# A hybrid decoder step on one core: attention heads taken in another order of steps, and one page more scored among the last pairs

## The chip, the cores and the metric

The kernel runs on one core of one Trainium2 chip. The metric is the device time of one execution in microseconds (us). TensorE (PE in the rows, its weight loads PEld) multiplies matrices into PSUM; VectorE (DVE), ScalarE (ACT) and GpSimd (POOL) work on tiles; SyncE (SP) and POOL issue most of the DMAs.

## The reference

One layer of a decoder for 512 prompt rows and 8 sample rows, model width 2048. Cut to what the change touches:

```python
q, k, v, lf                      # 8 heads of 128, 512 rows; q and k after an RMS norm, lf a log forget value
F = cumsum(lf)
s = q @ k.T * 128 ** -0.5 + F[:, None] - F[None, :]      # in blocks of 128 queries, causal
y = softmax(s) @ v
# for each of the 8 sample rows: the same over 2 pages of 128 cached keys and itself
s_sample = sum(q_row * cache_k[page_table[b]], -1) * scale + forget terms
```

Ahead of this stand the projections of the normalised input (`w_in`), behind it `w_proj_b`, `w_out` and a gated feed-forward part. Every product is made in three parts of reduced precision: weights and data are split into a high and a low tile (`wh`, `wl`, and so on), ACT casting the high one, DVE subtracting for the low one.

## The kernel before

**Order of the work.** Most products are "pairs": two weight chunks make seven products of 8 x 3 matmuls (about 2.9 us of TensorE each). `run_pairs` (L326) runs over steps `t`, seven to a unit; at each step it issues the small work that is due (`take`, `ahead`, and what the dictionary `late` has for `t`), then the product. A weight part is split two products ahead of its use. The units of the first mixer's late part are 23: step 161 is where they end, and `t0` is step 147. Engines T, V and S are wrapped by `Ordered` (L53; its line is L60, which is why most rows say L60): they keep the program's order. In the next stage G and Y (POOL and SP) keep it too.

**The stage around the change** (from L1618) is a loop over 16 half chunks of eight remaining gate columns, `for n, (j, e) in enumerate(halves)` (L1898), with 8 steps `k` in each: 128 steps of six matmuls. After the six matmuls of step `8 n + k` it runs what the dictionary `plan` holds for that step, in the order in which `put` (L1817) was called: first the heads in their order, then the sample rows' work. At k = 2 ACT casts the weights of the half after next, at k = 4 DVE makes their low part, at k = 3 SP loads those of four halves on.

**A head** has 13 steps (`HP`, L1832) and starts at step b = 1 + 13 hh. Its work: `f_load` and `f_roots` (SP: q, k and their two rows of roots, and v), `f_norm` (DVE), `f_forget` (a matmul, then ACT), `f_split` (ACT) and `f_split_low` (DVE) for q and k, `f_values` (4 transposes, then ACT) and `f_values_low` (DVE), `f_scores` for the four blocks (`fS`), `f_max` (DVE, then ACT's exponential), `f_scale` (DVE: reciprocal and multiply), three `f_turn` (transposes into `fPT`, then ACT's cast `fph`), three `f_turn_low` (DVE: `fpl`), four `f_attend` (`fy`), `f_result` (ACT). Block 3 is the longest and the last; every `f_turn` reads a part of it. The tail of a head lies beside the start of the next one.

**Buffers.** All these PSUM results, and those of the sample rows, share four one-bank buffers (`pm`, L75, `mm_ps`). `st` tiles are 33, `pt` tiles 9, weight tiles `raw` 7, `wh` and `wl` 3 each.

**Pages.** The sample rows' scores are 16 pages' worth of work. `s_load` (L1437) fetches a broadcast query row `qb` (SP) and two key tiles by indirect DMA (POOL); `s_scores` (L1457) has two parts. A page with i < `PT` (L1447) lies in three `pt` tiles, and each part is a multiply and a reduction over 512 columns. A later page lies in one `raw` tile: part 0 is a multiply, part 1 a reduction over 1024 columns. Pages 0 to 3 are scored among the last pairs (`pages`, L1574), the other twelve in the stage, 11 steps to two pages, from step 8 to step 70.

**Later**, at L2210, the pairs of `w_out` have at step 9 (second unit, its third product) `log_exp` (L108), which has ACT load the table with the logarithm and the exponential.

Of the kernel before, what the change touches and what calls it, by code (L numbers as in the profile page):

```python
# [18 lines left out]
P = 128  # L19
# [4 lines left out]
N = SEQ + NS  # L24
# [39 lines left out]
def tile_hybrid_step(ctx: ExitStack, tc: tile.TileContext, I, O):  # L64
    nc = tc.nc
    S, V, G, T, Y = nc.scalar, nc.vector, nc.gpsimd, nc.tensor, nc.sync
# [13 lines left out]
    def nm(s):  # L80
        uid[0] += 1
        return f"{s}{uid[0]}"
# [4 lines left out]
    def mconst(shape, name, dt=F32, tag=None):  # L87
        return cm.tile(shape, dt, tag=tag or name, name=name)

    def st(name, dt=F32):  # L90
        return sp.tile([P, 528], dt, tag="s", name=nm(name))

    def pt(name, dt=F32):
        return sp.tile([P, 528], dt, tag="p", name=nm(name), bufs=9)

    def tiny(name):
        return tp.tile([P, 32], F32, tag="tiny", name=nm(name), bufs=12)
# [7 lines left out]
    def dram(shape, name):  # L105
        return dp.tile(shape, F32, tag=nm(name), name=nm(name))
# [48 lines left out]
    def raw_tile():  # L155
        return wp.tile([P, 1024], F32, tag="raw", name=nm("raw"), bufs=7)

    def wraw(src):
        raw = raw_tile()
        with tc.high_priority():  # L160
            nc.sync.dma_start(raw[:, :src.shape[1]], src)
        return raw
# [12 lines left out]
    def on(f, *a):  # L175
        return lambda: f(*a)
# [51 lines left out]
    def parts_of(t):  # L228

        return t[:, :HN], t[:, HN:2 * HN]  # L230
# [496 lines left out]
    for i, (c0, n) in enumerate(phases):  # L727
        todo = {j: [] for j in range(NPRE)}

        def put(j, f, *a):  # L730
            todo[j].append(on(f, *a))
# [13 lines left out]
        if i + 1 < len(phases):  # L745
            a, b = range(c0 + n, c0 + 2 * n)
# [113 lines left out]
    for e in range(2):  # L860
        t = mconst([P, NS * NPG], f"idxf{e}")
# [5 lines left out]
    def gather(dst, src, idx):  # L867
        return G.indirect_dma_start(dst, None, src, bass.IndirectOffsetOnAxis(ap=idx, axis=0))
# [348 lines left out]
    H = mheads = follows = None  # L1217
# [95 lines left out]
    dv = dram([FH, P, N], "dv")  # L1313
# [123 lines left out]
    def s_load(i):  # L1437
# [3 lines left out]
        Y.dma_start(qb[:, :512], dqf[e, b].partition_broadcast(P))  # L1441
        kps = [pt("kp")[:, :512] for _ in range(NPG)] if i < PT else raw_tile().rearrange("p (g n) -> p g n", g=NPG)
        W.k[i] = qb, kps
        for g in range(NPG):
            gather(kps[g] if i < PT else kps[:, g], I["cache_k"], idx_h[e][:, b * NPG + g:b * NPG + g + 1])

    PT = 5  # L1447

    class Pages:
        pass  # L1450
# [6 lines left out]
    def s_scores(i, part):  # L1457
        e, b = divmod(i, NS)
        qb, kps = W.k[i]
        if i < PT:  # L1460
            V.tensor_tensor(kps[part], kps[part], qb[:, :512], op=ALU.mult)
# [15 lines left out]
    dss, drr = dram([2, FH, N], "dss"), dram([2, FH, N], "drr")  # L1477
# [4 lines left out]
            Y.dma_start(t[:, :N], src)  # L1482

    def f_roots(H):
        H.rq, H.rk, H.v = st("fi"), st("fi"), st("fi")
        for t, src in ((H.rq, drr[0, H.i].partition_broadcast(P)), (H.rk, drr[1, H.i].partition_broadcast(P)),
                       (H.v, dv[H.i])):
            Y.dma_start(t[:, :N], src)

    def f_norm(H):  # L1490
        for t, w, r in ((H.q, qwc, H.rq), (H.k, nkw, H.rk)):
            V.scalar_tensor_tensor(t[:, :N], t[:, :N], w, r[:, :N], op0=ALU.mult, op1=ALU.mult)
        H.rq = H.rk = None
# [5 lines left out]
    for hh in range(FH):  # L1499
        H = Head()  # L1500
        H.i, H.p, H.pt, H.fs, H.sm, H.tp = hh, [], {}, {}, {}, {}
        heads.append(H)
    H = None
# [27 lines left out]
    t0, tq = 7 * (len(units) - 2), 7 * (2 * FH)  # L1531
# [3 lines left out]
    def gate_load(n):  # L1535
        if n < len(halves):
            j, e = halves[n]
            gw[n] = raw_tile()
            Y.dma_start(gw[n], I["w_in"][1 + 24 + 24 + KC + j][:, e * 1024:(e + 1) * 1024])
# [13 lines left out]
    def gate_split(n):  # L1553
        gate_cast(n)
        gate_low(n)
# [3 lines left out]
    def upper():  # L1559
# [8 lines left out]
    late_steps = {7 * (KC + 2): late_turn, tq + 2: root_load, tq + 5: root_make, tq + 8: rows_load, tq + 11: rows_make,  # L1568
                  tq + 15: lambda: (s_rows(0), s_rows(1)), t0 + 9: lambda: (hX.pop(5), f_load(heads[0]), f_roots(heads[0]), upper()),
                  t0 + 8: lambda: (gate_load(0), gate_load(1)),  # L1570
                  t0 + 10: lambda: (gate_load(2), gate_load(3)), t0 + 12: on(s_load, 4),
                  t0 + 11: on(gate_split, 0), t0 + 13: lambda: (gate_split(1), f_norm(heads[0]))}
    late_steps = {t: [f] for t, f in late_steps.items()}
    pages = ((133, 143), (140, 150), (147, 157), (152, 162))  # L1574
    for i, (a, b) in enumerate(pages):
        for t, f in ((a, on(s_load, i)), (b, on(s_scores, i, 0)), (b + 2, on(s_scores, i, 1))):
            late_steps.setdefault(t, []).append(f)
# [6 lines left out]
    for j in range(KC):  # L1584
# [11 lines left out]
        if j < NG:  # L1596
            t = sgs[j]
            V.tensor_tensor(z2(t), acc, z2(t), op=ALU.mult)
        else:
            t = pt("pao")  # L1600
# [11 lines left out]
    for n in (7, 4):  # L1612
        for i in range(8):
            t = st("hf", F32R)
# [4 lines left out]
    G, Y = (Ordered(tc, e) for e in (G, Y))  # L1619
# [70 lines left out]
    def f_max(H, i):  # L1690
        n = (i + 1) * P
        ps = H.fs.pop(i)
        s = st("fs")
        sm = tiny("sm")
        V.tensor_tensor_reduce(s[:, :n], ps[:, :n], H.nf[:, :n], -1.0, 3e38, ALU.add, ALU.min, sm[:, 0:1])
        S.activation(s[:, :n], s[:, :n], AF.Exp, bias=sm[:, 0:1], scale=-1.0, accum_out=sm[:, 1:2])
        H.p.append(s)
        H.sm[i] = sm
        if i == NB - 1:
            H.q = H.k = H.v = H.qr = H.kr = H.nf = None  # L1700

    def f_scale(H, i):
        n = (i + 1) * P
# [129 lines left out]
    for hh, H in enumerate(heads):  # L1833
        b = 1 + hh * HP
        if hh:
            put(max(1, b - 11), f_load, H)
            put(max(2, b - 8), f_roots, H)
            put(b, f_norm, H)
        put(b + 1, f_forget, H)
        put(b + 2, f_split, H)  # L1840
        put(b + 3, f_values, H)
        put(b + 4, f_split_low, H)
        put(b + 4, f_keys_out, H)
        put(b + 5, f_values_low, H)
        for s, i in ((8, 0), (9, 1), (11, 2), (12, 3)):
            put(b + s, f_scores, H, i)
            put(b + s + 1, f_max, H, i)
            put(b + s + 3, f_scale, H, i)
        for j in range(3):
            put(b + 17 + j, f_turn, H, j)  # L1850
            put(b + 18 + j, f_turn_low, H, j)
        for j in range(NB):
            put(b + min(21 + j, 23), f_attend, H, j)
        put(b + 24, f_result, H)
        put(max(100 + 3 * hh // 1, b + 25), y_split, hh)
        put(max(100 + 3 * hh // 1, b + 25) + 1, y_low, hh)
    put(3, s_offsets)
    put(5, s_keep)
    for i in range(4, 16):
        b = 8 + 11 * (i - 4) // 2  # L1860
        if i > 4:
            put(max(1, b - 11), s_load, i)
        put(b, s_scores, i, 0)
        put(b + 2, s_scores, i, 1)
# [8 lines left out]
    for n in range(8):  # L1873
        t = 83 + 5 * n
# [10 lines left out]
    H = None  # L1885
    mg = [None] * KC
# [37 lines left out]
    T, V, S, G, Y = nc.tensor, nc.vector, nc.scalar, nc.gpsimd, nc.sync  # L1924
# [6 lines left out]
    def hl_parts(pool, tag, src, n=N):  # L1931
        hi, lo = (pool.tile([P, 528], F32R, tag=tag, name=nm("mf")) for _ in range(2))
        S.copy(hi[:, :n], src[:, :n])
        V.tensor_tensor(lo[:, :n], src[:, :n], hi[:, :n].bitcast(F32), op=ALU.subtract)
        return [(hi[:, o:o + HN], lo[:, o:o + HN]) for o in (0, HN)]
# [10 lines left out]
    def quarters(i):  # L1946
        return [t[:, o:o + HN] for t in (mg[i], mg[8 + i]) for o in (0, HN)]

    def m_sums(i, part):
        b11, b12, b21, b22 = quarters(i)  # L1950
        if part == 0:
            V.tensor_tensor(b11, b11, b12, op=ALU.subtract)
            V.tensor_tensor(b12, b22, b12, op=ALU.subtract)
        if part == 1:
            V.scalar_tensor_tensor(b22, b22, -1.0, b11, op0=ALU.mult, op1=ALU.subtract)
        if part == 2:
            V.scalar_tensor_tensor(b21, b22, -1.0, b21, op0=ALU.mult, op1=ALU.subtract)

    def m_parts(i, n):
        if n == 5:  # L1960
            mX[5][i], mX[7][i] = hl_parts(hp, "hl", mg[i])
            return
        f = quarters(i)[3 if n == 6 else 2]
        t = (st if i == 7 else pt)("mf", F32R)
        hi, lo = mX[n][i] = parts_of(t)
        S.copy(hi, f)
        V.tensor_tensor(lo, f, hi.bitcast(F32), op=ALU.subtract)
        if i < 7:
            G.dma_start(dxf[i + 8 * (n == 4)][:, :N], t[:, :N])
# [182 lines left out]
    def load2(u, o, e):  # L2152
        raws[u, o, e] = wraw(I["w_fi"][u + o * KF][:, e * 1024:(e + 1) * 1024])
# [21 lines left out]
    for n in (6, 4):  # L2175
        for i in range(7):
            t = st("mf", F32R)
# [3 lines left out]
    def fetch_xa(cs):  # L2181
        for c in cs:
            xa[c] = st("xa")
            nc.sync.dma_start(xa[c][:, :N], dxa[c])
# [18 lines left out]
    def first_weights(o):  # L2203
        ws.append(parts2(0, o, 0))
        load2(1, o, 0)
# [1 line left out]
    r2 = st("rr")  # L2207
    run_pairs(units, {
        0: lambda: (m_sums(7, 0), m_sums(7, 1)), 1: lambda: (m_parts(7, 5), m_sums(7, 2)),
        4: lambda: (m_parts(7, 4), mg.clear()), 9: log_exp, 50: lambda: fetch_xa(range(8)), 51: lambda: (load2(0, 0, 0), load2(0, 1, 0)), 53: tot_parts,  # L2210
        54: lambda: (first_weights(0), half_squares(1)), 55: lambda: (first_weights(1), half_norm(1))}, 0)
    mX = units = None

# [444 lines left out]
    for k in range(0, KC, 2):  # L2658
        t = 7 * (4 + 2 * k)
# [114 lines left out]
```

## Time and profile before

| | before |
|---|---|
| median of 3 runs (lowest to highest) | 2844.78 us (2842.81 to 2845.59) |
| the profiled execution, its own time | 2842.11 us |
| span of the profiled execution | 2840.4 us |
| PE busy | 2808.3 us (99%) |
| DVE busy | 2172.9 us (76%) |
| ACT busy | 1365.0 us (48%) |
| POOL busy | 382.1 us (13%) |
| mean granted TensorE clock | 0.999 |

Times in the views count from the start of the span. A row of the timeline has start, duration, engine, line, operation, the tile written and those read, shapes and a count; in brackets stands how long the engine had been idle before it and what ended that. Rows of the same kind that follow one another are merged. Two DVE operations in a row overlap by some 0.1 us, so that the distance of two starts is a little less than a duration.

### The profile page before, as it was taken

To read this page: it belongs to the slowest core of one execution; us is meant where nothing else is said; L and a number is where in the kernel's file an instruction comes from. 1 tells how busy PE (TensorE), PEld (TensorE's weight loads), DVE (VectorE), ACT (ScalarE), POOL (GpSimd) and SP (SyncE) were. 2 spreads that over 40 slices of the span, in tenths; PEclk is the share of its full clock that TensorE was granted. 3 is DMA by queue.
4 is the path that set the end of the run, shared out by engine and by line. 5 is a ranking of instruction groups with operands and counts; after the bars stand their busy time and mean duration, and the time that the engine had idled before them with its cause. 6 is when DMAs were issued, how large, how long until landed. Compare 5 with 4: busy or idle time off the path is not lost.

```text
span 2840.4 us, 57479 instructions
## 1 busy us (share of the span) xinstructions
PE 2808.3 (99%) x23270; PEld 2699.6 (95%) x23270; DVE 2172.9 (76%) x3300; ACT 1365.0 (48%) x2143; POOL 382.1 (13%) x659
## 2 busy tenths in 40 slices
PE   8999999999999999999999999999999999999999
PEld 6888998999999999899999999999999999999999
DVE  5986764576677789578888888787788888788787
ACT  4335553455555455445555444444444445444543
POOL 0001111201100132302211101011110101100100
PEclk9999999999999999999999999999999999999999
DMA  9946657855555578776672434444443346755753
GB/s 339 315 142 204 227 183 257 293 172 188 186 186 176 185 232 271 242 226 217 214 250 79 149 131 142 138 147 148 141 135 130 128 138 187 205 161 170 183 161 104
DMA packets 227842, 531.42 MB, mean 187 GB/s; under 512 B 30368, under 2 KB 83088, under 8 KB 227576
## 3 DMA queue, kind: packets, MB, share of 16 engines
q1 hardware_dynamic: 189600, 431.15, 46.8%
q0 software_dynamic: 37536, 96.38, 11.2%
q8 instruction: 182, 2.98, 0.4%
q14 instruction: 84, 0.69, 0.1%
q10 hardware_dynamic: 440, 0.23, 0.0%
HBM read 451.28 MB, written 72.92 MB: 185 GB/s over the span
## 4 chain that ended last, share of the span: by engine, by line
PE 90%; DVE 5%; DMA 2%; ACT 2%; issue 1%; SPq 0%; POOL 0%; ACTq 0%; DVEq 0%
PE x L60 35%; PE y L60 17%; PE z L60 9%; PE fo L60 4%; PE pa L213 3%; PE pb L213 3%; PE pre L60 3%; PE gate L60 2%; PE mo L213 2%; PE adp L60 2%; PE mv L213 2%; DMA ar<-in_w_ada 1%; DVE wl L60 1%; PE adp L409 1%; ACT wh L60 1%
## 5 line engine op out<-in xcount | busy, mean ns | idle before, releaser
L60 DVE TENSOR_TENSOR wl<-raw,wh 128x1024 fp32r<-128x1024 f32 (+1 forms) x696 | 838.7, 1206 | 358.4 <-ACT wh L60 355.7
L60 ACT CAST wh<-raw 128x1024 fp32r<-128x1024 f32 (+1 forms) x696 | 720.7, 1037 | 776.0 <-DVE raw L60 397.7
L60 PE MATMUL x<-bf,wh 128*128 128x260 f32 x2624 | 474.8, 282 | 0.0
L60 DVE TENSOR_TENSOR raw<-raw,raw 128x1024 f32<-128x1024 f32 x347 | 423.5, 1220 | 6.0
L60 PEld LDWEIGHTS x<-bf,wh 128*128 128x128 f32 x2624 | 403.2, 188 | 0.0
L60 PE MATMUL x<-bf,wl 128*128 128x260 f32 x1312 | 369.4, 282 | 0.0
L60 PEld LDWEIGHTS x<-bf,wl 128*128 128x128 f32 x1312 | 247.0, 188 | 0.0
L60 PE MATMUL y<-bf,wh 128*128 128x260 f32 x1312 | 239.1, 283 | 0.0
L60 PE MATMUL x<-hf,wh 128*128 128x260 f32 x1104 | 203.0, 284 | 0.0
L60 PEld LDWEIGHTS y<-bf,wh 128*128 128x128 f32 x1312 | 201.5, 188 | 0.0
L60 PE MATMUL x<-ff,wh 128*128 128x260 f32 x1024 | 186.1, 283 | 0.0
L60 PE MATMUL y<-bf,wl 128*128 128x260 f32 x656 | 185.1, 282 | 0.0
L60 PEld LDWEIGHTS x<-hf,wh 128*128 128x128 f32 x1104 | 169.7, 188 | 13.4 <-DVE tt L60 6.7
L60 PEld LDWEIGHTS x<-ff,wh 128*128 128x128 f32 x1024 | 157.5, 188 | 0.0
L60 PE MATMUL x<-hf,wl 128*128 128x260 f32 x552 | 155.7, 282 | 0.0
L168 DVE TENSOR_TENSOR wl<-raw,wh 128x1024 fp32r<-128x1024 f32 x68 | 83.1, 1223 | 88.7 <-ACT wh L167 87.4
L60 PE MATMUL x<-ff,wl 128*128 128x260 f32 x512 | 144.4, 282 | 0.0
L167 ACT CAST wh<-raw 128x1024 fp32r<-128x1024 f32 x68 | 71.3, 1049 | 135.1 <-DMA raw<-in_w_in 42.1
L60 PE MATMUL fo<-fe,wh 128*128 128x260 f32 x768 | 125.4, 284 | 1.0 <-DVE fo L60 0.7
L60 PEld LDWEIGHTS y<-bf,wl 128*128 128x128 f32 x656 | 123.3, 188 | 0.0
L60 PE MATMUL z<-bf,wh 128*128 128x260 f32 x656 | 119.1, 282 | 0.0
L60 PEld LDWEIGHTS fo<-fe,wh 128*128 128x128 f32 x768 | 105.8, 188 | 2.6 <-DVE fo L60 2.1
(640 smaller groups left out, 6984.5 us busy)
## 6 DMA issues: line engine op xcount, KB each, us to landing
raw<-in_w_fi SPq DMA_DIRECT2D x176, 512.0 KB
raw<-in_w_in SPq DMA_DIRECT2D x155, 512.0 KB
ar<-in_w_ada SPq DMA_DIRECT2D x192, 256.0 KB
raw<-in_w_ada SPq DMA_DIRECT2D x96, 512.0 KB
raw<-in_w_fo SPq DMA_DIRECT2D x64, 512.0 KB
raw<-in_w_out SPq DMA_DIRECT2D x32, 512.0 KB
raw<-in_w_fo SPq DMA_DIRECT2D x32, 384.0 KB
dff<-cc POOLq DMA_DIRECT2D x44, 260.0 KB
```

What stands on the lines that cost most here:

```text
L60: return lambda *a, **k: self.tc.keep_in_program_order(getattr(self.eng, op)(*a, **k))
L167: S.copy(wh[:, :n], raw[:, :n])
L168: V.tensor_tensor(wl[:, :n], raw[:, :n], wh[:, :n].bitcast(F32), op=ALU.subtract)
L213: T.matmul(acc[:, z, :HN], a[:, o], b[:, z * HN:(z + 1) * HN], start=(k == 0 and i == 0), stop=(k == K - 1 and i == 2))
L409: ins = T.matmul(ps[32 * g:32 * g + 32, :], cs[:, k, :], w, start=first, stop=last, tile_position=(0, 32 * g))
```

## The change

It moves a head's steps, moves the load of v into a step of its own, scores page 4 among the last pairs, spaces the remaining eleven pages by six steps, and moves `log_exp` by two steps.

```diff
-    PT = 5
+    PT = 6
...
     def f_roots(H):
-        H.rq, H.rk, H.v = st("fi"), st("fi"), st("fi")
-        for t, src in ((H.rq, drr[0, H.i].partition_broadcast(P)), (H.rk, drr[1, H.i].partition_broadcast(P)),
-                       (H.v, dv[H.i])):
+        H.rq, H.rk = st("fi"), st("fi")
+        for t, src in ((H.rq, drr[0, H.i].partition_broadcast(P)), (H.rk, drr[1, H.i].partition_broadcast(P))):
             Y.dma_start(t[:, :N], src)
+
+    def f_load_values(H):
+        H.v = st("fi")
+        Y.dma_start(H.v[:, :N], dv[H.i])
...
-                  t0 + 10: lambda: (gate_load(2), gate_load(3)), t0 + 12: on(s_load, 4),
+                  t0 + 10: lambda: (gate_load(2), gate_load(3)), t0 + 12: on(s_load, 5),
...
-    pages = ((133, 143), (140, 150), (147, 157), (152, 162))
+    pages = ((133, 140), (139, 146), (145, 152), (151, 158), (156, 162))
...
         put(b + 1, f_forget, H)
+        put(b + 1, f_load_values, H)
         put(b + 2, f_split, H)
-        put(b + 3, f_values, H)
         put(b + 4, f_split_low, H)
         put(b + 4, f_keys_out, H)
-        put(b + 5, f_values_low, H)
-        for s, i in ((8, 0), (9, 1), (11, 2), (12, 3)):
+        for s, i in ((6, 0), (7, 1), (9, 2), (10, 3)):
             put(b + s, f_scores, H, i)
             put(b + s + 1, f_max, H, i)
             put(b + s + 3, f_scale, H, i)
+        put(b + 11, f_values, H)
+        put(b + 12, f_values_low, H)
         for j in range(3):
-            put(b + 17 + j, f_turn, H, j)
-            put(b + 18 + j, f_turn_low, H, j)
+            put(b + 16 + j, f_turn, H, j)
+            put(b + 17 + j, f_turn_low, H, j)
         for j in range(NB):
-            put(b + min(21 + j, 23), f_attend, H, j)
-        put(b + 24, f_result, H)
+            put(b + min(20 + j, 22), f_attend, H, j)
+        put(b + 23, f_result, H)
...
-    for i in range(4, 16):
-        b = 8 + 11 * (i - 4) // 2
-        if i > 4:
+    for i in range(5, 16):
+        b = 8 + 6 * (i - 5)
+        if i > 5:
             put(max(1, b - 11), s_load, i)
...
-        4: lambda: (m_parts(7, 4), mg.clear()), 9: log_exp, 50: lambda: fetch_xa(range(8)), 51: lambda: (load2(0, 0, 0), load2(0, 1, 0)), 53: tot_parts,
+        4: lambda: (m_parts(7, 4), mg.clear()), 11: log_exp, 50: lambda: fetch_xa(range(8)), 51: lambda: (load2(0, 0, 0), load2(0, 1, 0)), 53: tot_parts,
```

`f_max` no longer drops `H.v`, which lives until `f_values`.

## Rows read from the trace of the kernel before

**Rows 1.** Largest wait of PE in the stage: releaser; us, times, longest.

```profile
PE fPT L60 <- DVE fs L60: 2.0, 2, 1.1
```

**Rows 2.** Stretches: us; busy us of PE, PEld, DVE, ACT, POOL; clock, DMA share, GB/s.

```profile
1000.00:1020.10 20.10, 20.10 (x171) 20.10 (x170) 16.44 (x19) 9.81 (x15) 4.20 (x6) 1.00 0.48 162
...
1075.50:1090.80 15.30, 15.30 (x122) 14.55 (x121) 14.90 (x31) 8.43 (x21) 6.57 (x6) 1.00 0.97 326
...
1131.00:1202.70 71.70, 69.23 (x533) 57.76 (x532) 39.34 (x117) 34.23 (x81) 28.23 (x28) 1.00 0.68 230
```

**Rows 3.** Timeline of PE: the first turn of each of the first five heads.

```profile
1061.92 0.49 PE L60 MATMUL fPT<-ident,fs 128*128 128x128 f32 x3
1063.48 0.33 PE L60 MATMUL fPT<-ident,fs 128*128 128x128 f32 x1 [1.07 <-DVE fs L60]
...
1078.40 0.63 PE L60 MATMUL fPT<-ident,fs 128*128 128x128 f32 x4
...
1093.64 0.60 PE L60 MATMUL fPT<-ident,fs 128*128 128x128 f32 x4
...
1109.28 0.49 PE L60 MATMUL fPT<-ident,fs 128*128 128x128 f32 x3
1110.67 0.33 PE L60 MATMUL fPT<-ident,fs 128*128 128x128 f32 x1 [0.90 <-DVE fs L60]
...
1125.60 0.81 PE L60 MATMUL fPT<-ident,fs 128*128 128x128 f32 x4
```

**Rows 4.** The scoring of pages on DVE: ns least/median/most, first and last start.

```profile
L60 DVE TENSOR_REDUCE sc<-raw x11: 1206/1210/1216, 1061.6 to 1128.3; 128x8 f32<-128x1024 f32 x11
L60 DVE TENSOR_REDUCE sc<-kp x10: 685/686/687, 994.8 to 1054.6; 128x4 f32<-128x512 f32 x10
```

**Rows 5.** Timeline of DVE: its first wait, and the second low part of the same five heads.

```profile
1053.65 0.29 DVE L60 CUSTOM_DVE_ANT_0 fs<-fS,nfb 128x128 f32<-128x128 f32 x1 [2.06 <-PE fS L60]
...
1068.21 0.88 DVE L60 TENSOR_TENSOR fpl<-fPT,fph 128x384 fp32r<-128x384 f32 x2
...
1083.10 0.88 DVE L60 TENSOR_TENSOR fpl<-fPT,fph 128x384 fp32r<-128x384 f32 x2
...
1098.26 0.55 DVE L60 TENSOR_TENSOR fpl<-fPT,fph 128x384 fp32r<-128x384 f32 x1
...
1114.51 0.56 DVE L60 TENSOR_TENSOR fpl<-fPT,fph 128x384 fp32r<-128x384 f32 x1 [0.34 <-ACT last L60]
...
1130.66 0.88 DVE L60 TENSOR_TENSOR fpl<-fPT,fph 128x384 fp32r<-128x384 f32 x2
```

**Rows 6.** Chain that ended last, from the second head's first turn: start, us, what.

```profile
1078.57 0.47 PE fPT L60 x4
1079.04 0.72 PE gate L60 x6
...
1082.58 0.69 PE fy L60 x3
1083.28 0.28 PE fS L60 x3
```

**Rows 7.** Timelines of SP, ACT and PE around the longest gap of the stage.

```profile
1144.09 15.63 SPq L161 DMA_DIRECT2D raw<-in_w_pb  x5
...
1149.40 0.48 ACT L60 CAST fph<-fPT 128x384 fp32r<-128x384 f32 x1 [4.57 <-remote]
...
1150.68 0.49 PE L60 MATMUL fS<-fi,fi 128*128 128x128 f32 x2 [1.76 <-issue]
```

**Rows 8.** Timelines of ACT and PE at the table load in the second pair of w_out.

```profile
1326.23 1.28 ACT L60 ACT_TABLE_LOAD   x1
...
1327.95 0.51 PE L60 MATMUL x<-mf,wh 128*128 128x260 f32 x2 [0.81 <-ACT tg L60]
```

**Rows 9.** Waits of SP's own queue in the stage, the largest.

```profile
SPq L60 <- DVE sm L60: 28.6, 6, 7.7
```

**Rows 10.** Chain that ended last: a query row of 256 KB, from issue to landing.

```profile
1108.78 3.39 DMA qb<-dqf
```

More of the change, by code (lines that the diff above doesn't have):

```diff
@@ L1699, in f_max @@
         if i == NB - 1:
-            H.q = H.k = H.v = H.qr = H.kr = H.nf = None
+            H.q = H.k = H.qr = H.kr = H.nf = None
     def f_scale(H, i):
```

## The prediction

> **What bounds the kernel now.** I read the waits of PE first, since PE is busy in 99% of the span: only idle time of PE, or work added to it, can move the end. The stage of the heads lies between about 1043 and 1203 us. Its largest wait is for DVE's scaled scores ahead of a turn, 2.0 us in two waits [rows 1]. The stretches say the same of the engines: between 1075.50 and 1090.80, one head long, DVE is busy for 14.90 of 15.30 us beside a full PE, so the two are equally loaded and DVE has no reserve; after the last page, from 1131.00, DVE is busy for only 39.34 of 71.70 us, and PE is idle for 71.70 - 69.23 = 2.47 us [rows 2]. The timeline of PE gives the two waits their places: 1.07 us in the first turn of head 0 and 0.90 us in that of head 3 [rows 3]. Of the 2.47 us, 1.76 us are one gap at 1150 us, behind an ACT that had stood for 4.57 us while five weight loads of w_pb were issued [rows 7]. Outside the stage, one wait bears on the change: 0.81 us of PE behind a table load of 1.28 us on ACT [rows 8]. All that the change can reach is thus 1.07 + 0.90 + 2.47 + 0.81 = 5.25 us. Two tenths of a per cent, which is about what a measurement of this kernel can tell from no change, are 5.7 us.
>
> **Part by part.** *A page moves out of the stage.* On DVE a late page is a multiply and a reduction over 1024 columns, 1.21 us each [rows 4], some 2.3 us with the overlap of neighbours. The stage scored twelve, now eleven: 2.3 us less DVE work between steps 8 and 70, or 0.45 us a head over five heads.
>
> *The same page is added to the pairs.* Two halves of a multiply and a reduction of 0.69 us each [rows 4], 2.7 us. A stretch of seven products in which two such halves already lie has DVE busy for 16.44 of 20.10 us and PE for all of it [rows 2]; with 3.66 us free it holds one more page, and over the last four units the change adds just one. The halves now fall on other products than before. A half pushes the next weight parts back by at most 1.4 us, and a part is made two products (5.7 us) ahead. I take 0; if that cover failed, it would cost at most those 1.4 us at each of ten places, 14 us, but no row of the pairs shows PE waiting, so I give that end no weight. Its last half, head 0's norm and the tail end 1.3 us later on DVE than before; head 0's first scores come two steps earlier, and DVE stood for 2.06 us waiting for just these [rows 5], so this is hidden too. The page's query row (SP) and two gathers (POOL) are issued six to seven products ahead instead of ten, far over the 3.39 us that a query row took [rows 10].
>
> *The turn gets a step more.* From `f_scale` of block 3 to the first `f_turn` there were two steps, now three (b + 13 to b + 16), and from the scores to the turn six instead of five. A step is six gate matmuls, 0.72 us, and with a turn in it 0.47 us more [rows 6]: 1.19 us. The waits it has to cover are 1.07 and 0.90 us [rows 3]. I take them as gone: -1.97 us. Bounds: 0 (DVE slips along) and -1.97.
>
> *The scores come nearer to the previous head's low parts.* This is where the stall may go. The second block's scores (`fS`, b + 7) need a PSUM buffer. Four are shared; in the new order the tiles are `fPT` three times, `fS` of block 0, `fy`, `fS` of block 1, so the last takes the buffer of the second `fPT`, which is free when DVE has made the second `fpl`. PE comes there as follows: from the first turn to the end of the first `fy` are 1082.58 + 0.69 - 1078.57 = 4.70 us, and the first block's `fS`, 0.28 us, now lies between them: 4.98 us [rows 6]. In the trace the second `fpl` ended (start plus 0.55 us) after the first turn's start by: head 0, 1068.21 + 0.55 - 1061.92 less the wait of 1.07 = 5.77 us; head 1, 5.25; head 2, 5.17; head 3, 4.89 (less its 0.90); head 4, 5.61, less the 0.21 by which its turn took 0.81 and not 0.60 us: 5.40 [rows 3, 5]. Over 4.98 us that is 0.79, 0.27, 0.19, 0 and 0.42 us, together 1.67 us of new waits. The page taken out gives back up to 0.45 us a head, which would leave 0.34. I take 1.2 us, nearer to the upper value, as DVE's low part of q and k (1.2 us) now stands between the first and the second `fpl`. Bounds: 0.3 to 1.7 by these rows; what more would be is a rival below.
>
> Beside this the Trainium skill ("Perfetto Trace Analysis", section "Identifying Performance Opportunities") says that a gap repeating over a stretch on the engine that should be saturated can mean that there is too little SBUF or PSUM for the next tile. In this trace the gaps are two, and a DVE multiply ended both, so the trace does not show that yet; by the page the new order would repeat a gap at each head, which is the slower rival.
>
> *Values later.* Load of v, four transposes, two ACT copies and a DVE subtraction go to b + 11 and b + 12; they are needed at b + 20, and PE's work is the same. The load is issued by SP at b + 1 instead of b - 8, ten steps ahead of its transposes, at least 7.2 us at 0.72 each; it needs 3.39 us by [rows 10], and if it hit SP's longest wait too, 7.7 us [rows 9], it would be late by up to 4 us once. The next head's loads of q and k stand behind it, with eleven steps' lead. I take 0.
>
> *The table load* moves from the third to the fifth product of its unit, behind a cast of weights that has two products' lead instead of ahead of a copy that the next product waits for: -0.81 us [rows 8]. Bounds: 0 and -0.81.
>
> *The gap at 1150 us* [rows 7]: the change doesn't touch what I take to be near it, w_pb's loads. I leave it; bounds -2.47 us and, if it came twice, +2.47.
>
> **Sum.** -1.97 + 1.2 - 0.81 = -1.6 us (-1.58). Against the profiled execution's own time, 2842.11, that makes 2840.5 us; that execution lies 2.7 us under the median of the runs shown, 2844.78, and just under the fastest. The forecast is for the median: 2843.2 us.
>
> **Rivals.** *The gap at 1150 us goes as well* (chance 0.20): it hangs on which instruction of the chain falls together with the five loads, and PE's order around it shifts by a step or two. For it: ACT's wait has no counterpart at the other heads. Against: the loads come when weight buffers come free, which hardly changes. 2843.2 - 2.47 = 2840.7 us.
>
> *DVE stays the bound* (0.22): the two turns no longer wait, but the same 1.97 us turn up at `fS` and `fy`, because DVE's 14.90 us of 15.30 shrink by only 0.45. Only the table load pays: 2844.78 - 0.81 = 2844.0 us, and 2845 with the upper bounds of the waits.
>
> *Slower through PSUM* (0.06): at each of seven heads the second `fpl` comes later than now by one half page (1.13 us net), because a page's half or a weight part falls between it and the first, and `fS` of block 1 waits for its buffer. Price: 7 x (1.67/5 + 1.13) = 10.2 us, less 1.97 and 0.81: +7.4, 2852.2 us. It decides where the second `fpl` ends over 6 us after the first turn began. For it: no slack in these rows; against: the largest was 5.77 us, with more pages.
>
> *Nearly every wait goes* (0.07): 2844.78 - 5.25 = 2839.5 us, with half of its spread under 2839.1, the bound of 0.2%.
>
> The forecast itself has 0.45. That the change does not do what it says is excluded by its text, as every step is written out by hand.
>
> **How the numbers follow.** The likeliest case is 2843.2 us. The range runs from the case in which the gap goes (2840.7, less about 0.8 for the spread of runs, which is 2.8 us from lowest to highest) to the case of a bound DVE at the upper ends (2845, with the same spread and 1 us for the bounds set to 0): 2839.9 to 2846.8 us. Left out are the slower rival, the lower half of the last one and the tails of the others. Faster by over 0.2% needs practically all 5.25 us and some: 0.05. Slower: the PSUM rival, 0.06. Within: 0.89.
>
> **What would show it.** Right: no wait of `fPT` for `fs`; waits of `fS` for `fpl` or of the same size without a named releaser, under 0.5 us each; no wait of the second w_out pair for `tg`; DVE busy below 14.9 of 15.3 us a head. Wrong: a wait of `fS` over 1 us at every head; a transpose of v waiting for its load; PE waiting in the pairs around 960 to 1043 us for `wl` or `tt`; the 1.76 us gap gone or doubled.

## The result and the profile after

The changed kernel takes 2856.34 us (median of 6 runs, 2855.47 to 2863.22) against 2842.79 us beside it (6 runs, 2841.88 to 2845.59): ratio 1.0050, 95% interval 1.0037 to 1.0063. It is slower by 13.5 us, outside the range of the prediction and on the side that had 0.06. Below, `r_after_2` and `e9_gaps_first` each had one execution of over 7000 us instead of about 2850, which the ratios leave out.

The first lines of its page: PE is busy for 99% as before, but the span is 14.2 us longer.

```profile
span 2854.6 us, 57504 instructions
PE 2816.3 (99%) x23270; PEld 2706.4 (95%) x23270; DVE 2175.1 (76%) x3302; ACT 1365.6 (48%) x2143; POOL 381.7 (13%) x659
```

The stretches say where. First the kernel before, then the changed one; the columns are those of [rows 2].

```profile
940.00:1043.00 103.00, 103.00 (x863) 102.95 (x862) 83.17 (x99) 49.43 (x70) 22.97 (x32) 1.00 0.55 175
1043.00:1203.00 160.00, 155.19 (x1197) 138.72 (x1196) 122.25 (x281) 84.73 (x195) 59.17 (x59) 1.00 0.82 268
```

```profile
940.00:1043.00 103.00, 101.84 (x852) 101.64 (x852) 84.22 (x101) 49.84 (x71) 23.64 (x33) 1.00 0.59 189
1043.00:1203.00 160.00, 147.99 (x1099) 132.29 (x1098) 117.89 (x261) 80.05 (x181) 58.42 (x58) 0.97 0.75 247
1106.00:1113.00 7.00, 5.35 (x41) 4.93 (x40) 2.97 (x6) 1.26 (x5) 4.00 (x5) 1.00 0.87 300
1113.00:1119.80 6.80, 5.64 (x28) 5.24 (x26) 6.20 (x10) 3.98 (x9) 0.00 (x0) 0.50 0.36 130
1160.80:1164.20 3.40, 3.03 (x13) 2.93 (x14) 1.88 (x9) 1.10 (x4) 0.00 (x0) 0.50 1.03 406
```

In the 160 us of the heads PE ran 98 matmuls fewer. At 155.19 / 1197 = 0.130 us each, its standing still for 155.19 - 147.99 = 7.2 us more is worth 55 of them. For 6.8 and 3.4 us the granted clock was 0.50, the level of 1.2 GHz; PE was busy for 5.64 + 3.03 = 8.67 us of them, and half of that, 4.3 us, is lost, worth 33. Together that is 88 of the 98 by this estimate. Ahead of the first of these stretches PE had been busy for only 5.35 of 7.00 us. From the first gate matmul to the first of `pb`, which I call the stage from here on, it takes 172.0 us instead of 159.9.

PE's waits from 940 to 1215 us in the changed kernel (releaser; us, times, longest):

```profile
PE fS L60 <- DVE fpl L60: 5.3, 4, 3.7
PE sOT L60 <- issue: 2.0, 1, 2.0
PE gate L60 <- issue: 1.6, 2, 0.9
PE fPT L60 <- DVE fs L60: 1.5, 2, 1.2
PE x L60 <- DVE tt L60: 1.2, 1, 1.2
PE sPT L60 <- DVE sm L60: 0.7, 1, 0.7
```

The largest is the one the prediction feared, `fS` for `fpl`, but 3.7 of its 5.3 us are a single wait, the others 0.70, 0.46 and 0.46 us. The 3.7 us begin earlier. The timeline of POOL, PE, ACT and DVE of the changed kernel around that wait, and around a similar place a head earlier:

```profile
1104.67 0.23 PE L60 MATMUL fS<-mask_f,identb 128*128 128x128 bf16 x1
...
1104.94 0.56 DVE L60 CUSTOM_DVE_ANT_0 fs<-fS,nfb 128x384 f32<-128x384 f32 x1 [0.67 <-issue]
...
1105.18 0.94 POOL L60 DMA_INDIRECT vp<-in_cache_v,idx  x1 [0.30 <-issue]
...
1106.21 0.23 PE L60 MATMUL fS<-mask_f,identb 128*128 128x128 bf16 x1
...
1106.43 1.04 POOL L60 DMA_INDIRECT vp<-in_cache_v,idx  x1 [0.30 <-issue]
...
1107.05 0.60 PE L60 MATMUL vtp<-ident,fi 128*128 128x128 f32 x4
...
1109.41 0.40 PE L60 MATMUL gate<-hh,wl 128*128 128x260 f32 x2
...
1109.91 0.69 DVE L60 CUSTOM_DVE_ANT_0 fs<-fS,nfb 128x512 f32<-128x512 f32 x1 [3.27 <-PE gate L60]
...
1110.27 0.95 POOL L60 DMA_INDIRECT vp<-in_cache_v,idx  x1 [0.30 <-issue]
...
1112.75 0.45 PE L60 MATMUL gate<-hh,wh 128*128 128x260 f32 x2 [0.93 <-issue]
1112.85 0.48 ACT L60 CAST fvh<-vtp 128x384 fp32r<-128x384 f32 x1 [1.38 <-remote]
...
1154.05 0.38 PE L60 MATMUL fPT<-ident,fs 128*128 128x128 f32 x2
...
1158.48 0.94 POOL L60 DMA_INDIRECT vp<-in_cache_v,idx  x1 [0.31 <-issue]
1160.29 0.37 ACT L60 CAST fph<-fPT 128x256 fp32r<-128x256 f32 x1 [6.80 <-remote]
1160.70 0.42 DVE L60 TENSOR_TENSOR fpl<-fPT,fph 128x256 fp32r<-128x256 f32 x1 [4.23 <-issue]
...
1161.17 0.58 PE L60 MATMUL fS<-fkh,fqh 128*128 128x256 f32 x1 [3.69 <-DVE fpl L60]
```

Read the pairs of a PE row and the DVE or ACT row that needs its result. The first is normal: the mask's matmul ends at 1104.67 + 0.23 = 1104.90, DVE starts 0.04 us later. The next block's ends at 1106.44, and DVE, idle for 3.27 us, starts 3.47 us later. The transposes of v end at 1107.65; ACT starts 5.20 us later. The transposes `fPT` end at 1154.43; ACT, idle for 6.80 us, starts 5.86 us later, and `fpl` and `fS` hang on it. PE itself wasn't late: it went on with gate matmuls in order up to 1109.41, and the starts of those are recorded. What came late is the news that PE had finished. I call this a late report. The end of a PE record is modelled, and the Trainium skill ("Perfetto Trace Analysis", section "Summary: the profiler window per engine type") says the same: that end is estimated, and the way of the semaphore's news to the other engines isn't in that record. In the first pair above it takes 0.04 us, at the late places 2.4 to 5.9.

The trace also keeps the times at which semaphores were updated, which no view prints. From 940 to 1240 us, 18 of the 247 updates of PE's semaphore stand 0.5 to 5.6 us behind the last PE record that makes one, 17 of them at the four places below; of DVE's 298 updates and ACT's 194 none stands more than 0.5 us behind. What is late is thus PE's update itself, and only PE's.

The late reports of the changed kernel lie at four places, and at each of them POOL is in an unbroken run of gathers (`DMA_INDIRECT`) or has just ended it, one in 1.25 us for the most part: 1049 to 1057, 1103 to 1111, 1150 to 1159, 1190 to 1199 us. In both cases shown, the last `DMA_INDIRECT` row of the run lies 1.8 and 2.6 us ahead of ACT's start. The kernel before has two such places. In the first ACT starts 3.13 us behind the transposes of v, with no wait of PE behind it; the second is the gap of [rows 7]: ACT's 4.57 us "remote" are 3.53 us behind the end of its `fPT`, and the next `fPT` was reported 5.43 us late. The kernel before, PE and ACT:

```profile
1108.12 0.60 PE L60 MATMUL vtp<-ident,fi 128*128 128x128 f32 x4
1111.85 0.48 ACT L60 CAST fvh<-vtp 128x384 fp32r<-128x384 f32 x1 [2.10 <-PE fPT L60]
...
1145.26 0.60 PE L60 MATMUL fPT<-ident,fs 128*128 128x128 f32 x4
...
1146.42 0.38 PE L60 MATMUL fPT<-ident,fs 128*128 128x128 f32 x2
...
1152.23 0.37 ACT L60 CAST fph<-fPT 128x256 fp32r<-128x256 f32 x1 [2.19 <-PE fS L60]
```

### The profile page after: what moved, and what is told of

It is laid out like the page before. It is cut to its first block, busy times and chain, and to the rows that moved or that the text cites. A ratio compares the mean times of both kernels' runs of the same rounds, so it can differ in the third digit from the quotient of the medians.

```text
span 2854.6 us, 57504 instructions
## 1 busy us (share of the span) xinstructions
PE 2816.3 (99%) x23270; PEld 2706.4 (95%) x23270; DVE 2175.1 (76%) x3302; ACT 1365.6 (48%) x2143; POOL 381.7 (13%) x659
## 4 chain that ended last, share of the span: by engine, by line
PE 90%; DVE 4%; DMA 2%; ACT 2%; issue 1%; SPq 0%; another core or an unknown queue 0%; POOL 0%; DVEq 0%; ACTq 0%
PE x L60 34%; PE y L60 17%; PE z L60 8%; PE fo L60 4%; PE pa L213 3%; PE pb L213 3%; PE pre L60 3%; PE mo L213 2%; PE gate L60 2%; PE adp L60 2%; PE mv L213 2%; DMA ar<-in_w_ada 1%; PE adp L409 1%; DVE wl L60 1%; PE mq L213 1%
```

## The experiments

Each is timed beside runs of the kernel before on the same chip (chips 0, 1, 3 and 12 in five series). "Late" are starts of ACT or DVE, after idle time, 2 us or more behind the end of the PE record they need, in the profiled execution. "Gather" is `DMA_INDIRECT` on POOL.

**The halves of the change (chip 0).** The heads alone: `f_load_values` and the new steps of a head, pages and `log_exp` as before. The pages alone: five pages, every six steps, and `log_exp` at 11.

```diff
e1_heads
+        put(b + 1, f_load_values, H)
+        for s, i in ((6, 0), (7, 1), (9, 2), (10, 3)):
+            put(b + 16 + j, f_turn, H, j)
e2_pages
+    pages = ((133, 140), (139, 146), (145, 152), (151, 158), (156, 162))
+        b = 8 + 6 * (i - 5)
+        ... 11: log_exp, ...
```

> The new order of a head alone (with the later load of v); the pages and the table load as before. Theory A (the order of a head brings the loss, because PE's scores and turns now fall together with long runs of gathers on POOL): 2850 to 2858 us, with the stage of the heads 8 to 13 us longer than before. Theory B (the pages bring it, through DVE and the gathers' new places): 2841 to 2845 us.

> The pages (five among the last pairs, eleven every six steps) and the later table load; the order of a head as before. Theory A: 2841 to 2844 us, the wait of 1.16 us of the last pair for tt there, the wait of 0.8 us in w_out gone, the heads' stage within 2 us of before. Theory B: 2850 to 2858 us.

Measured: heads 2848.93 us, ratio 1.0031 (1.0019 to 1.0042), stage 163.9 us; pages 2845.70, ratio 1.0021 (1.0011 to 1.0030), stage 156.3. Neither half pays, and neither time lies in the range of either theory. With the heads alone `fS` waits for `fpl` 4.4 us at five places, the longest 1.8, and behind that one the clock is at half for 3.4 us: with twelve pages still in the stage, the waits of the PSUM rival do appear, though under 1 us at four of the five places. With the pages alone, PE waits 1.2 us for `tt` in the pairs. Neither shows a late report on this chip (none of the 273 updates of PE's semaphore in the heads alone from 940 to 1240 us stands more than 0.5 us behind its record), and the kernel before takes only 2839.90 us on it. The changed kernel itself was not run on this chip.

**No gathers of value pages (chip 0).** In both kernels the 32 gathers of value pages become plain DMAs of as many bytes; they read fixed rows, so the part of the outputs that rests on the value pages is other data.

```diff
-        gather(W.v[i][:, :512], I["cache_v"], idx_h[e][...])
+        G.dma_start(W.v[i][:, :512], I["cache_v"][i * P:(i + 1) * P, :])
```

> The changed kernel with the 32 gathers of value pages replaced by plain transfers of as many bytes from fixed rows, issued by POOL at the same places (the sample rows' values are then those of other pages). Theory A1 (the runs of gathers hold up what PE reports): the waits of 3 to 7 us of ACT and DVE at about 1106, 1155 and 1196 us go, and so does the half clock behind them: 2844 to 2850 us. Theory A2 (the bytes in flight hold it up, whichever way they are asked for): within 2 us of the changed kernel, 2854 to 2858 us. Theory C (the waits are PE's own, of the order of its work): 2856 us too.

> The kernel before with the same replacement. Theory A1: ACT's wait of 4.6 us at 1145 us and the gap of 1.76 us go: 2835 to 2840 us. Theories A2 and C: 2842 to 2844 us.

Measured: the changed kernel 2842.78 us, ratio 1.0010 (1.0000 to 1.0019); the kernel before 2840.60, ratio 1.0000 (0.9990 to 1.0009). Without gathers the change costs 2.2 us, not 13.5. The kernel before gains nothing from plain DMAs on this chip, against theory A1. Whether the gathers or the chip made the difference was still open here.

**Both kernels again, and gaps between the gathers (chip 1).** `r_before` and `r_after` are the two kernels; `e5_after_gaps` puts a memset of 0.54 us on POOL ahead of each gather of a value page, so that one comes in about 1.8 us; `e6_table` is the kernel before with `log_exp` at 11.

```diff
e5_after_gaps
+        G.memset(W.v[i][:, :512], 0.0)
         gather(W.v[i][:, :512], I["cache_v"], idx_h[e][...])
e6_table
-        ... 9: log_exp, ...
+        ... 11: log_exp, ...
```

> The kernel before once more, for its trace on the chip of this call: equal to the runs of before beside it, within 0.1%. Theory A1 (what PE reports comes late in a long run of gathers) expects its wait of 4.6 us of ACT after the first product with value pages again; if that wait is missing, it is no property of the program alone.

> The changed kernel once more, on the same chip as the rest of this call. If its loss is of the program alone (PSUM waits and pages), it stands 12 to 15 us over before, as in the first comparison, with half clock in the heads' stage. If part of it hangs on the chip or on one execution (the three waits of 3 to 7 us of ACT and DVE), it stands 4 to 10 us over before and the trace lacks those waits.

> The changed kernel with a memset of 0.5 us on POOL ahead of each gather of value pages, so that two gathers never follow one another at once; results as before. Theory A1: the late reports of PE go, 5 to 11 us less than the changed kernel. Theory A2 (bytes in flight) and theory C (PE's own order): within 2 us of the changed kernel, or later by what a late gather costs.

> The kernel before with only the table load moved by two steps. Prediction's term: the wait of 0.81 us of the second w_out pair goes, 0.5 to 1.2 us less than before. Rival: ACT's cast behind the load is late instead, no change.

Measured: `r_before` 1.0000 (0.9990 to 1.0010), late 3.48 and 5.38 us at the same two `fPT` as before and 3.22 us at a `vtp`, stage 160.3; `r_after` 2854.36, 1.0037 (1.0023 to 1.0051), late at three places by up to 5.6 us, two stretches of 3.4 us at half clock, stage 167.6; with gaps 2848.23, 1.0016 (1.0006 to 1.0026), nothing late, no half clock, stage 161.3. The memsets are more work for POOL, and yet they save 6.1 us. PE's waits in the version with gaps are what the change leaves when reports are prompt:

```profile
PE fS L60 <- DVE fpl L60: 1.8, 4, 0.9
PE x L60 <- DVE tt L60: 1.2, 1, 1.2
PE sPT L60 <- DVE sm L60: 0.7, 1, 0.7
PE sO L60 <- DMA vp<-in_cache_v,idx: 0.5, 1, 0.5
PE fPT L60 <- DVE fs L60: 0.2, 1, 0.2
```

The table load: 2842.80, ratio 0.9997 (0.9987 to 1.0006). PE's 0.8 us for `tg` are gone in its trace, but so small a gain isn't resolved in the time.

**Which gathers, and does the kernel before gain too (chip 3).** `e9_gaps_first` has the memset ahead of the first five gathers only (`if i < 5`); `e7_before_gaps` is the kernel before with all memsets and `log_exp` at 11; `e8_gaps_page` is `e5_after_gaps` with the halves of the fourth early page a product earlier:

```diff
-    pages = (..., (151, 158), (156, 162))
+    pages = (..., (150, 157), (156, 162))
```

> The changed kernel a third time, the base for the next three on their chip. Where ACT and DVE stand for 3 to 6 us each at three places again: 10 to 13 us over before. Where a chip does not show these (e2's trace, with the same gathers, had none): 3 to 6 us over before.

> The changed kernel with the memset of 0.5 us ahead of the first five gathers of value pages alone (those that POOL issues at about 1105 us). Theory A1: the wait of 3.3 us of DVE at 1110 and of 1.4 us of ACT at 1113 go, and the half clock behind them; those at 1160 and 1197 stay: 2 to 6 us less than the changed kernel. Theory C (order of PE's work) and chance in the alignment of POOL and the rest: no change, or all of them change.

> The kernel before with the memset ahead of every gather of value pages and the later table load. Theory A1: the 4.6 us of ACT and the 1.7 us gap of PE at 1150 go: 3 to 5 us less than before, and about 1 us for the table: 2838 to 2840 where before is 2844. Rival: gathers now late for the products, or no change but for the table: 1 us less at most, or slower.

> The changed kernel with the memsets and with the fourth page's halves one step earlier (157 and 159 instead of 158 and 160). If the wait of 1.16 us for tt is of those two steps, it goes: 1 us less than with the memsets alone, 3 to 4 us over before. If any step there costs the same, no change.

Measured: the changed kernel again 1.0037 (1.0023 to 1.0050), late at four places, stage 172.3. Gaps in the first five gathers alone: 2850.26, 1.0024 (1.0014 to 1.0034), stage 164.8; the place near 1105 is gone, those near 1056, 1150 and 1190 stay (up to 2.3, 5.5 and 2.9 us). The late reports thus follow the run of gathers next to them. The kernel before with gaps: 2844.23, 1.0003 (0.9993 to 1.0012); its late reports and the 1.7 us gap go, but turns wait 2.7 us for `fs` and `sO` 0.9 us for value pages: no gain, where 3 to 5 us were expected. So removing late reports need not pay where other waits stand behind them. The fourth page a product earlier: 2846.23, 1.0010 (1.0000 to 1.0019), and PE's 1.2 us for `tt` are gone in its trace; the ratio isn't told apart from the 1.0016 of the memsets alone.

**Gathers, bytes or the chip (chip 3 again).** One more run of the changed kernel; the plain DMAs of `e3_after_plain` and the heads alone of `e1_heads`, same texts, now on a chip with late reports; and a memset of 8 columns instead of 512.

```diff
e12_short_gap
+        G.memset(W.v[i][:, :8], 0.0)
```

> The changed kernel once more, as the reference of the three runs beside it on this chip. If what PE has finished is reported late in every execution of it: ratio 1.004 to 1.005, a stage of 167 to 172 us, two to four places where DVE or ACT start 2 us or more after the end of the PE record that they wait for. If that depends on the chip: on a chip without it, no such place, and a ratio of 1.002 or less, like the version with gaps.

> The changed kernel with the 32 gathers of value pages replaced by plain DMAs of the same bytes (of fixed rows, so that the output parts that rest on the value pages are other numbers). Theory, that the runs of gathers delay the reports: on a chip where the changed kernel beside it shows late reports, none over 1.5 us here, and a stage of 157 to 161 us, about 8 us or more under it. Rival, that the bytes or their number do it: late reports of 2 us or more stay, and the stage stays above 164 us.

> The kernel before with the new order of a head alone, its pages as they were. Theory, that which runs of gathers fall together with the heads' chain decides: where the changed kernel beside it shows late reports, this one shows at least those of the kernel before (about 3.5 and 5.4 us near 1147), as the gathers run as before, beside its waits of fS for fpl of about 4.4 us: stage 164 to 168. Rival, that the new order of the heads is by itself the cause: late reports at the three or four places of the changed kernel, stage of 170 or more. If it is the spacing of the pages: as the kernel before, no more than one place.

> The changed kernel with a memset of 8 columns on POOL ahead of each gather of a value page instead of one of 512. If any instruction between two gathers is enough: no late report over 1.5 us and a ratio of 1.0015, as with the long memset (stage 161). If it is the rate of gathers (one in 1.25 us; with the long memset one in 1.8): one in about 1.4 to 1.5 us here, and some late reports of 1 to 3 us stay, stage 162 to 167.

Measured: changed kernel 2852.05, 1.0033 (1.0020 to 1.0046), late at four places by up to 5.6 us, stage 165.2. Plain DMAs beside it: 2843.50, 1.0000 (0.9990 to 1.0010), nothing late, stage 157.1: it is the gathers, not their bytes (POOL's queue moved the same 2880 packets and 9.44 MB from 1100 to 1215 us in both). The heads alone: 2858.96, 1.0053 (1.0035 to 1.0071), stage 175.3, against 163.9 for the same text on chip 0. The timelines of this one text, ACT and PE at the same instruction, show the difference; first on chip 0, then on chip 3.

```profile
1152.56 0.38 PE L60 MATMUL fPT<-ident,fs 128*128 128x128 f32 x2
1152.98 0.37 ACT L60 CAST fph<-fPT 128x256 fp32r<-128x256 f32 x1 [0.98 <-PE fPT L60]
```

```profile
1157.42 0.38 PE L60 MATMUL fPT<-ident,fs 128*128 128x128 f32 x2
1157.90 1.16 POOL L60 DMA_INDIRECT vp<-in_cache_v,idx  x1 [0.30 <-issue]
...
1161.87 0.95 POOL L60 DMA_INDIRECT vp<-in_cache_v,idx  x1 [0.30 <-issue]
1162.85 0.37 ACT L60 CAST fph<-fPT 128x256 fp32r<-128x256 f32 x1 [5.98 <-remote]
```

0.04 us on chip 0, 5.05 on chip 3, with the same eight gathers at the same spacing around it. Full queues don't explain it either: on chip 0 the DMA engines were busy for 0.82 and then 1.03 of the time from 1152.5 to 1161.0. No late report in any of these traces stands away from a run of gathers, and the chip (or something else that differs between these series) decides whether a run delays.

The short memset: 2846.92, 1.0015 (1.0005 to 1.0024), stage 165.2. One gather in 1.33 us; the places near 1150 and 1190 are gone, but the profiled execution, the slowest of the ten, still has reports late by 2.3 us near 1056, where the gathers are of keys and have no memset, and by 4.97 us near 1108, with the clock at half for 6.8 us behind that one. So neither "any instruction between" nor the rate alone is confirmed.

**The halves again (chip 12).** The pages alone, same text as `e2_pages`, and `e1_heads` with the memsets of 512 columns.

> The kernel before with the changed pages (five among the pairs, eleven every six steps) and the moved table load, its heads in the old order. If the spacing of the pages alone puts runs of gathers where the heads' chain waits for PE: late reports of 2 us or more at two places or more, ratio of 1.003 or more, a stage of 163 us or longer. If the order of the heads decides, as the heads alone were 15.5 us slower than before on one chip: at most the places of the kernel before (one, near 1147 us), ratio about 1.002, as on the first chip (5.8 us slower), 1.2 us of it PE's wait for tt in the pairs.

> The new order of a head alone (old pages), with a memset of 0.5 us on POOL ahead of each gather of a value page. Theory: the late reports go, what is left are the waits of fS for fpl of about 4.4 us that DVE's page in each head causes: stage about 164 us, ratio 1.002 to 1.003, on this chip as on the first. Rival, that the order of the heads costs by itself what it cost without gaps: ratio 1.004 or more, stage over 168 us.

Measured: pages 2848.12, 1.0020 (1.0011 to 1.0030), late at the same two `fPT` as the kernel before (3.52 and 5.45 us) and nowhere else, with 3.4 us at half clock behind them, stage 159.6; heads with gaps 2852.87, 1.0034 (1.0020 to 1.0048), nothing late, stage 169.3, PE waiting 4.3 us for `fpl`, 1.3 for value pages and 1.1 for `fs`, with 3.4 us at half clock. That stage is the rival's, over 168 us, and not the 164 of the theory: with the old pages the new order of the heads loses time without any late report. It also brings the extra late places on chip 3; the pages bring no late report of their own. Their loss is elsewhere: 1.2 us for `tt`, and a slower step of matmuls long after the stage. Windows of 800 us with the same products: before, pages alone, changed kernel.

```profile
1600.00:2400.00 800.00, 799.94 (x6696) 787.14 (x6696) 644.23 (x808) 374.07 (x492) 91.71 (x199) 1.00 0.44 142
```

```profile
1600.00:2400.00 800.00, 799.94 (x6659) 787.14 (x6658) 640.69 (x799) 372.16 (x486) 90.30 (x197) 1.00 0.44 140
```

```profile
1600.00:2400.00 800.00, 800.00 (x6691) 787.40 (x6690) 642.85 (x793) 370.60 (x480) 88.96 (x195) 1.00 0.43 139
```

PE is full in all three, but the pages alone fit 37 matmuls fewer, 4.4 us, and the changed kernel 5, 0.6 us. All three traces hold 23270 matmuls, so no record is missing on one side. The counts of `e2_pages` and `e13_pages_again` on two chips are equal, those of the kernel before differ by one, so the step belongs to the program's text. Its cause is open.

## Why the prediction was wrong, and where it was right

**The step that failed** is "The gap at 1150 us": "the change doesn't touch what I take to be near it, w_pb's loads. I leave it; bounds -2.47 us and, if it came twice, +2.47". Five loads on SP stood beside ACT's 4.57 us in [rows 7], and I took neighbours in time for the cause. ACT waited for a result that PE had finished 3.53 us before, and the row hinted at it: "remote" names no engine. The releaser to look for was POOL's run of gathers at that time, which stands in none of the rows I read. Seen so, the gap isn't one event but a price that a handover from PE to ACT or DVE can pay when it falls into such a run. The new order of a head puts more of them there: in its four profiled executions the changed kernel has three or four such places, up to 5.9 us late, where the kernel before has two, of which one holds PE up. That is +7.2 us of standing PE, net of the waits that the change took away, which "came twice" underrates threefold, and the half clock behind it, 4.3 us, for which the sum had no term at all. Together 11.5 us, close to the stage's 172.0 - 159.9 = 12.1 and most of the 13.5.

That the gathers cause it on those chips is shown by three edits that leave PE, ACT and DVE as they are: gaps (-6.1 us), gaps in one run only (that place alone goes), plain DMAs (-8.6 us, 2852.05 to 2843.50). Why a run of gathers holds PE's reports up, and why not on chip 0, isn't shown.

**"The same page is added to the pairs ... I take 0"** was wrong by 1.2 us. A half of the fourth page stood on DVE ahead of the `tt` that PE needed: 0.69 us of `kp` and 0.69 of its reduction from 1039.66, then `tt`, and PE started at 1041.55. The changed kernel, DVE and PE:

```profile
1039.66 0.69 DVE L60 TENSOR_TENSOR kp<-kp,qb 128x512 f32<-128x512 f32 x1
1040.38 0.69 DVE L60 TENSOR_REDUCE sc<-kp 128x4 f32<-128x512 f32 x1
1040.98 0.42 DVE L60 TENSOR_TENSOR tt<-x,tt 128x260 f32<-128x260 f32 x1
...
1041.55 0.48 PE L60 MATMUL x<-hf,wh 128*128 128x260 f32 x2 [1.16 <-DVE tt L60]
```

The argument looked at weight parts, made two products ahead; `tt` has no such lead. The last section of the prediction named this wait as a sign, and `e8_gaps_page` removes it by moving a half by one product.

**Terms that held.** The turns' waits go from 2.0 to 0.2 us in the version with gaps (forecast 0); in the changed kernel 1.5 us are there, 1.2 of them behind a late report. The new waits of `fS` for `fpl` are 1.8 us there and about 1.9 in the changed kernel without the late one (forecast 1.2, bounds 0.3 to 1.7): the mechanism was right, and the size just over its upper bound. Its working has a slip, too: the path of PE was counted from 1078.57 [rows 6], where a row of the chain starts behind the end of the work before it, and the ends of `fpl` from the turn's own start, 1078.40 [rows 3]. From one start the path is 5.15 us and not 4.98, and the rows give 0.62 + 0.10 + 0.02 + 0.25 = 0.99 us and not 1.67, about half of what came. The table load's 0.81 us go as worked out. Values later cost nothing that a trace shows: no transpose of v waited for its load. DVE's 14.90 of 15.30 us became 14.45 between the same two times, though 15.16 of 15.30 from 1087.0 on: less work, not yet a reserve.

**What the sum would have had to be without late reports** is read from the two kernels with plain DMAs, where the forecast of -1.6 us meets 2842.78 - 2840.60 = +2.2. The times don't resolve such terms (the interval of each ratio is 0.1% to either side, 2.8 us); the traces have them. Of the 3.8 us, 1.2 are the wait for `tt`; 0.7 a wait of `sPT` for `sm` that the working had not seen at all (the transposes of the page scores come behind the softmax on DVE; it is there in every version with the new heads and in none without); 0.3 the waits of `fS` (1.5 against 1.2); and 0.8 that could not be won, since the turns of the kernel before then wait 1.2 and not 2.0 us. That is 3.0; for the other 0.8 a slower step of matmuls, 11 fewer in 800 us there, is a candidate that isn't shown.

**The rivals.** "Slower through PSUM" gave 2852.2, near the result for the wrong reason: its sign, a wait over 1 us at every head, didn't appear, and the one long wait came from ACT's late `fph`. Its mechanism is real, though, where the pages stay: 4.4 and 4.3 us at five and four places with the heads alone (`e1_heads`, `e14_heads_gaps`). The gap at 1150 neither went nor doubled in the sense of that rival; it moved and multiplied.

No version beat the kernel before: the best was the table load alone, 0.9997, which is not told apart from no change.

## What to carry to other kernels

When ACT or DVE starts long after the end of the matmul it needs, and PE has gone on meanwhile, subtract the two times before looking for a cause among neighbours, and look at what POOL does in those microseconds: an order of the work that puts a tight chain of handovers into a run of gathers may pay several us a time. Spread gathers out, or put them where PE has products queued that wait for nobody, and measure on more than one chip, as here the same text had late reports on one chip and none on another. Check also that no other wait takes the place of the one removed. A stall of PE of a few us costs more than itself when the granted clock falls behind it, as it did here for 3.4 or 6.8 us at a time.

## What the runs showed of the hardware that was not expected

- Reports of PE's results that take 2 to 6 us instead of 0.04, within or just behind runs of gathers one in 1.25 us, while DVE's and ACT's semaphore updates stay prompt; in the same text on another chip 0.04 us, and none of 2 us or more when the gathers of value pages come one in 1.8 us or as plain DMAs.
- Half of the clock (1.2 GHz) for 3.4 or 6.8 us at a time behind places where PE had stood, after 5.35 us busy of 7.00 in the changed kernel, and in `e1_heads`, without late reports, behind a wait of 1.8 us. Of two traces whose longest gap in the stage is 1.7 us, `e13_pages_again` shows 3.4 us of it and `r_before` none.
- The step of the same matmuls, with PE full, differs by the program's text: 6696, 6691 and 6659 in 800 us.
